# Gate and up in one 512-column product, convolution weights taken one pair at a time, rotary angles started after the convolution

## The chip, the cores and the metric

The kernel runs on one core of a Trainium2 chip. The metric is the device time of one execution in microseconds (us), the median of several runs. TensorE is called PE in the rows, the scalar engine ACT, the vector engine DVE, GpSimd POOL, and SyncE SP; SP issues nearly all loads from DRAM.

## What is computed

A decoder of two layers on 256 tokens of width 1024, all in float32. The parts that the change touches:

```python
def short_conv_mixer(h, w_in, w_conv, w_out):      # layer 0
    b_gate, c_gate, u = jnp.split(h @ w_in, 3, axis=-1)
    z = c_gate * u
    conv = lax.conv_general_dilated(z, w_conv[:, None, :], ...)   # 3 taps, each channel by itself
    return (b_gate * conv) @ w_out

def swiglu(h, w_gu, w_down):                       # both layers, D_FF = 2816
    g, u = jnp.split(h @ w_gu, 2, axis=-1)
    return (jax.nn.silu(g) * u) @ w_down

def rope_cos_sin(positions):                       # used by the attention of layer 1
    ang = positions[..., None] * inv_freq
    return jnp.cos(ang)[:, :, None, :], jnp.sin(ang)[:, :, None, :]
```

Around them stand RMS norms, an attention to a memory of 256 tokens in each layer (keys and values from the memory), and a causal attention in layer 1. Most of the work is the product of 256 tokens with weight matrices: 3 M weights in the convolution's `w_in`, 5.8 M in each layer's `w_gu`.

## The kernel before

**Three products for one.** Every float32 number is split in a part `hi` that TensorE reads exactly and a rest `lo`. A product is then hi by lo, lo by hi and hi by hi, summed in PSUM. Activations are split once. Weights stream: a 512 KB chunk is loaded to one of 5 `raw` buffers, ACT casts it to `hi`, DVE subtracts to get `lo`, and the pair stays in one of 10 buffers until its products are issued. The load of a chunk waits for the `lo` of the chunk five places ahead of it, which frees the raw buffer.

**Two forms.** Where the output has features on the partitions (`mm_cols`: the convolution's `cu` and `pb`, most of the gate and up products `gu`), a weight block is loaded into the array, and one product of 512 columns covers the activations' hi and lo; a second of 256 columns covers the weight's lo. Where the output has tokens on the partitions (`mm_rows`, `gate_up_rows`), 128 tokens are loaded and the weights stream through in three products (`mm3`). The gate and up products of the first two pairs of feature blocks (`ROW_PAIRS` = 2, `jp` 0 and 1) are made in the rows form in each layer, for the tokens of half 0 and then of half 1, so that half 0 can start before half 1 of the FFN's input is normed. There each `mm3` has 256 columns: 8 blocks `k` of the gate, then 8 of the up part, for 2 pairs and 2 halves, which is 2 x 2 x 2 x 8 x 3 = 192 products in a layer. `turn` then makes silu(gate) x up and transposes it back (`pt_g`). The normed input itself is brought to features by transposes (`pt_h`).

**The order of the work** is written by the Python program, instruction by instruction, for engines that each run their queue in order. A `Clock` models when each engine would be done. `side.poll()` after each product lets side jobs (generators that yield the time they want to wait) issue a step, and lets `Feed.pump` issue a cast or a subtraction of the next chunk, if the model has the engine free and its input there. `feed.take(name)` hands out a chunk, and issues at once its cast and subtraction, and those of the chunks ahead of it, where the pump has not done so. `hold` and `grab` wait for one of two PSUM tiles of a kind.

**The convolution** (`short_conv`) has four blocks `jp` of 256 features, in two groups `jj` each. A group is 8 products of 512 columns with `wc` (to one PSUM tile `cu`), 8 with `wu` (to the other), one with `wb` (to `pb`), 24 of 256 columns with the lo of the three, and the last seven with `wb`: 24 of 512 and 24 of 256. ACT and DVE then add the halves of the two `cu` tiles to `conv` tiles in SBUF, and the tiles come free for the next group. All six chunks of a block are taken at its head. The input of the convolution is `mix`: each half of the normed x is transposed (`pt_h`), cast (ACT `mix`) and subtracted (DVE `mix`). Into the first group also falls the job `tables`, which loads gains and the taps of the convolution (`g_rows`, `cw_rows`), transposes them on PE (`pt_c`) and copies them to SBUF.

**The angles** (`angles`) are a side job started ahead of the convolution: a DMA of the positions (`pos_i`), some ten small DVE operations on 32 columns (`ang`, `turns`, `cosang`), and four Sin on ACT (`cs`), ahead of which ACT loads its table for Sin.

Of the kernel before, what the change touches and what calls it, by code (L numbers as in the profile page):

```python
# [19 lines left out]
P = 128  # L20
D = 1024
KD = D // P
T = 256
# [84 lines left out]
class Side:  # L108
# [47 lines left out]
    def hold(self, kind):  # L156

        free = self.free[kind]
        while not free or min(free) > self.clock.now:
            yield 0 if not free else min(free) - self.clock.now  # L160
        free.remove(min(free))
# [11 lines left out]
class Feed:  # L173
# [3 lines left out]
    def __init__(self, clock, items, load, high, low):  # L177
        self.clock, self.items, self.load, self.high, self.low = clock, items, load, high, low
        self.loaded = self.highs = self.lows = self.taken = self.freed = 0
        self.raw, self.ready = {}, {}  # L180
        self.hooks = {}
        self.limit = 5
# [16 lines left out]
    def next_low(self):  # L199
        n = self.lows  # L200
        self.low(self.items[n], self.raw.pop(n), *self.ready[n])
        self.lows += 1
        self.load_to(self.lows + RAWS)
# [51 lines left out]
def yoco_kernel(  # L255
# [51 lines left out]
    def tok(h):  # L307
        return slice(h * P, (h + 1) * P)
# [22 lines left out]
    def load(dst, src, queue=None):  # L331
        (queue or nc.sync).dma_start(dst, src)
        clock.free["dma"] = max(clock.free["dma"], clock.now + 1100)
        clock.note("dma", 1.43 * math.prod(dst.shape[1:]), [dst], [], 900)
# [11 lines left out]

    def load_chunk(it):
        raw = raws.tile([P, it["a"], it["b"]], F32, tag="raw", name=f"raw_{it['name']}")
        src = it["src"].rearrange("(a p) n -> p a n", p=P)
        n = it["b"] // it["pieces"]  # L350
        for i in range(it["pieces"]):
            load(raw[:, :, i * n:(i + 1) * n], src[:, :, i * n:(i + 1) * n])
        return raw
# [36 lines left out]
    def ffn_plan(l):  # L390
        steps, last = ffn_steps()
        plan = []
        for kind, jp in steps + [("down", jp) for jp in last]:
            if kind == "gu":
                plan += col_plan(f"wg{l}_{jp}", ffn_w_gu[l], jp * T)
                plan += col_plan(f"wu{l}_{jp}", ffn_w_gu[l], DFF + jp * T)
            else:
                for k in (2 * jp, 2 * jp + 1):
                    plan.append(dict(name=f"wd{l}_{k}", src=ffn_w_down[l][k * P:(k + 1) * P, :], a=1, b=D,
                                     gain=None, pieces=1, halves=2))  # L400
        return plan
# [206 lines left out]
    def start_rstd():  # L608
        yield 9000
# [194 lines left out]
    def angles():  # L804
# [6 lines left out]
        yield 15000  # L811
# [62 lines left out]
    def short_conv(act, into):  # L874
# [35 lines left out]
        for jp in range(4):  # L910
            wc, wu, wb = ([feed.take(f"{name}_{jp}_{g}") for g in range(2)] for name in ("wc", "wu", "wb"))
            for jj in range(2):
# [3 lines left out]
                for w in (wc, wu):  # L916
                    side.grab("gu")
                    cus.append(gu_tile("cu"))
                    mm_cols(cus[-1], act, w, jj, 0)
                pb = acc_tile("pb").rearrange("p (r t) -> p r t", r=2)  # L920
                mm_cols(pb, act, wb, jj, 0, (0,))
                for i, w in enumerate((wc, wu)):
                    mm_cols(cus[i], act, w, jj, 1)
# [119 lines left out]
    def swiglu(l, src, done, fine_end=False, at_end=None):  # L1043
# [21 lines left out]
        def gate_up_rows(jp, w, h):  # L1065
# [3 lines left out]
            for part in range(2):  # L1069
                for k in range(KD):  # L1070
                    act.need(k, (h,))
                    mm3(gu[:, part, :], act.parts(k, tok(h)), [r[:, k % 4, :] for r in w[part][k // 4]],
                        k == 0, k == KD - 1)
                    side.poll()
# [66 lines left out]
        first = [gu_w(jp) for jp in range(ROW_PAIRS)]  # L1141
# [195 lines left out]
    side.start(angles())  # L1337
    side.finish(x_job[0])
    short_conv(in_mix.act, in_mem0)
    memv0 = mem_values("memv0", mT0)  # L1340
# [28 lines left out]
```

## Time and profile before

| | before |
|---|---|
| median of 3 runs | 802.57 us (801.74 to 802.96) |
| profiled execution, its own time | 804.97 us |
| its span in the trace | 803.2 us |
| PE busy | 789.1 us (98%) |
| DVE, ACT busy | 532.7 us (66%), 436.8 us (54%) |
| mean granted TensorE clock | 0.993 of full speed |
| bytes moved, mean rate | 146.55 MB, 182 GB/s |

"Busy" of PE counts the time from a product's start to its modelled end, and products overlap; the distance of two starts tells more than a duration. A row in brackets `[2.20 <-DVE mix]` says that the engine sat idle for 2.20 us before the instruction, and that DVE's `mix` ended the wait. The granted clock of a stretch is given in parts of full speed.

### The profile page before, as it was taken

To read this page: it belongs to the slowest core of one execution; us is meant where nothing else is said; L and a number is where in the kernel's file an instruction comes from. 1 tells how busy PE (TensorE), PEld (TensorE's weight loads), DVE (VectorE), ACT (ScalarE), POOL (GpSimd) and SP (SyncE) were. 2 spreads that over 40 slices of the span, in tenths; PEclk is the share of its full clock that TensorE was granted. 3 is DMA by queue.
4 is the path that set the end of the run, shared out by engine and by line. 5 is a ranking of instruction groups with operands and counts; after the bars stand their busy time and mean duration, and the time that the engine had idled before them with its cause. 6 is when DMAs were issued, how large, how long until landed. Compare 5 with 4: busy or idle time off the path is not lost.

```text
span 803.2 us, 11672 instructions
## 1 busy us (share of the span) xinstructions
PE 789.1 (98%) x4477; PEld 690.6 (86%) x4477; DVE 532.7 (66%) x830; ACT 436.8 (54%) x727; POOL 17.8 (2%) x44
## 2 busy tenths in 40 slices
PE   8899999999999999999999999999999999999996
PEld 8888788898898888888888889888989988888885
DVE  5888788666756656665765667877757555665553
ACT  6656646565645445554655664556645544554442
POOL 0100001000000000000010000010000000000000
PEclk9999999999999999999999999999999999999999
DMA  9666685833536654666474535667344465466611
GB/s 332 196 191 213 215 269 190 280 136 105 173 97 224 213 185 157 188 212 208 153 236 172 170 106 168 226 206 243 119 121 155 156 212 180 158 203 214 209 55 53
DMA packets 91085, 146.55 MB, mean 182 GB/s; under 512 B 4941, under 2 KB 70549, under 8 KB 90773
## 3 DMA queue, kind: packets, MB, share of 16 engines
q1 hardware_dynamic: 90276, 142.92, 54.8%
q0 software_dynamic: 288, 2.10, 0.7%
q8 instruction: 35, 0.57, 0.3%
q10 hardware_dynamic: 464, 0.79, 0.3%
q14 instruction: 22, 0.17, 0.1%
HBM read 142.64 MB, written 3.15 MB: 182 GB/s over the span
## 4 chain that ended last, share of the span: by engine, by line
PE 88%; DMA 5%; DVE 3%; ACT 2%; issue 1%; SPq 0%; POOLq 0%; ACTq 0%; DVEq 0%
PE gu L315 30%; PE ff L315 14%; PE q_acc L315 6%; PE acc_memv L315 5%; PE acc_mo L315 5%; PE acc_memk L315 3%; PE acc_v L315 3%; PE acc_q L315 3%; PE acc_k L315 3%; PE acc_o L315 3%; PE acc_cout L315 3%; PE cu L315 2%; DMA raw_wu<-in_conv_w_in_dram 2%; PE po L315 2%; PE s L315 2%
## 5 line engine op out<-in xcount | busy, mean ns | idle before, releaser
L315 PE MATMUL ff<-hi_wd,guT 128*128 128x512 f32 (+1 forms) x352 | 107.6, 387 | 0.0
L103 DVE TENSOR_TENSOR gu_sb<-gu_sb,gu 128x256 f32<-128x256 f32 x72 | 30.1, 421 | 97.0 <-ACT gu_sb L103 96.2
L103 ACT COPY gu_sb<-gu 128x256 f32<-128x256 f32 x72 | 26.4, 371 | 101.6 <-PE gu L315 101.5
L315 PEld LDWEIGHTS ff<-hi_wd,guT 128*128 128x128 f32 x352 | 65.9, 188 | 12.2
L103 ACT CAST hi_wu<-raw_wu 128x1024 fp32r<-128x1024 f32 x52 | 54.6, 1050 | 33.5 <-DMA raw_wu<-in_ffn_w_gu_dram 23.0
L315 PE MATMUL gu<-ffn,hi_wg 128*128 128x512 f32 x288 | 71.9, 391 | 0.4 <-DVE gu_sb L103 0.4
L315 PE MATMUL gu<-ffn,hi_wu 128*128 128x512 f32 x288 | 71.2, 389 | 0.0
L315 PE MATMUL ff<-lo_wd,guT 128*128 128x512 f32 (+1 forms) x176 | 68.5, 389 | 0.0
L103 DVE TENSOR_TENSOR lo_wu<-raw_wu,hi_wu 128x1024 fp32r<-128x1024 f32 x52 | 62.8, 1219 | 4.6 <-ACT hi_wu L103 4.5
L315 PEld LDWEIGHTS gu<-ffn,hi_wu 128*128 128x128 f32 x288 | 54.1, 188 | 11.3
L315 PEld LDWEIGHTS gu<-ffn,hi_wg 128*128 128x128 f32 x288 | 53.6, 188 | 11.6 <-DVE gu_sb L103 0.8
L103 DVE TENSOR_TENSOR lo_wd<-raw_wd,hi_wd 128x1024 fp32r<-128x1024 f32 x44 | 53.1, 1219 | 0.0
L103 DVE TENSOR_TENSOR lo_wg<-raw_wg,hi_wg 128x1024 fp32r<-128x1024 f32 x44 | 52.2, 1219 | 0.7 <-ACT hi_wg L103 0.5
L103 ACT CAST hi_wd<-raw_wd 128x1024 fp32r<-128x1024 f32 x44 | 45.6, 1050 | 2.8 <-DMA raw_wd<-in_ffn_w_down_dram 2.8
L315 PE MATMUL acc_memk<-mT,hi_memk 128*128 128x256 f32 x256 | 46.7, 287 | 0.0
L103 ACT CAST hi_wg<-raw_wg 128x1024 fp32r<-128x1024 f32 x44 | 44.6, 1051 | 0.6 <-PE acc_mo L315 0.6
L315 PEld LDWEIGHTS gu<-ffn,lo_wg 128*128 128x128 f32 x288 | 39.3, 190 | 2.8
L315 PE MATMUL acc_mo<-hi_mo,oT_mem 128*128 128x512 f32 x128 | 41.2, 397 | 0.2 <-DVE oT_mem L103 0.2
L315 PE MATMUL gu<-ffn,lo_wu 128*128 128x256 f32 x288 | 40.4, 283 | 0.0
L315 PE MATMUL gu<-ffn,lo_wg 128*128 128x256 f32 x288 | 40.2, 282 | 0.0
L315 PE MATMUL acc_memv<-hi_memv,mT 128*128 128x512 f32 x128 | 39.7, 391 | 0.0
L315 PEld LDWEIGHTS acc_memk<-mT,hi_memk 128*128 128x128 f32 x256 | 39.5, 193 | 0.2
(230 smaller groups left out, 1722.3 us busy)
## 6 DMA issues: line engine op xcount, KB each, us to landing
raw_wg<-in_ffn_w_gu_dram SPq DMA_DIRECT2D x44, 512.0 KB, 5.7
raw_wu<-in_ffn_w_gu_dram SPq DMA_DIRECT2D x44, 512.0 KB, 3.6
raw_wd<-in_ffn_w_down_dram SPq DMA_DIRECT2D x44, 512.0 KB, 4.8
raw_memv<-in_mem_w_kv_dram SPq DMA_DIRECT2D x16, 512.0 KB, 4.9
raw_mq<-in_mem_w_q_dram SPq DMA_DIRECT2D x16, 512.0 KB, 5.3
raw_mo<-in_mem_w_o_dram SPq DMA_DIRECT2D x16, 512.0 KB, 5.4
raw_memk<-in_mem_w_kv_dram SPq DMA_DIRECT2D x14, 512.0 KB, 5.4
raw_wc<-in_conv_w_in_dram SPq DMA_DIRECT2D x8, 512.0 KB, 3.8
```

The lines of the kernel that those rows point to most:

```text
L103: return call(out, *args, **kw)
L315: nc.tensor.matmul(o, l, r, start=start, stop=stop)
```

## The change

It has five parts. (1) In the rows form, the chunks of a pair hold two blocks `k` with 256 gate columns and 256 up columns side by side (`pair_plan`, names `wr`), each loaded by two DMAs of 256 KB. One `mm3` of 512 columns per `k` replaces two of 256, and the chunks are taken as `k` reaches them. (2) `short_conv` takes `wc`, `wu` and `wb` of a block one after the other, each ahead of its first product. (3) The modelled clock lets a load start only when its raw buffer is freed (`emptied`), and has a slower rate for chunks of several blocks; `hold` looks a second time at the clock. (4) The job that norms the memory yields 7000 instead of 9000 ns. (5) `angles` is started behind the convolution and waits 4000 instead of 15000 ns.

```diff
     def hold(self, kind):
         free = self.free[kind]
-        while not free or min(free) > self.clock.now:
+        seen = None
+        while not free or min(free) > self.clock.now != seen:
+            seen = self.clock.now if free else None
             yield 0 if not free else min(free) - self.clock.now
...
         self.lows += 1
+        self.emptied = self.clock.last
         self.load_to(self.lows + RAWS)
...
-    def load(dst, src, queue=None):
+    def load(dst, src, queue=None, rows=True, freed=0.0):
         (queue or nc.sync).dma_start(dst, src)
-        clock.free["dma"] = max(clock.free["dma"], clock.now + 1100)
-        clock.note("dma", 1.43 * math.prod(dst.shape[1:]), [dst], [], 900)
+        clock.free["dma"] = max(clock.free["dma"], clock.now + 1100, freed + 1100)
+        clock.note("dma", (1.43 if rows else 1.9) * math.prod(dst.shape[1:]), [dst], [], 900)
...
+    def pair_plan(name, w, c0):
+        return [dict(name=f"{name}_{g}", a=2, b=2 * T, gain=None, pieces=1, halves=1,
+                     src=[w[g * 256:(g + 1) * 256, c:c + T] for c in (c0, DFF + c0)]) for g in range(4)]
...
-            if kind == "gu":
+            if kind == "gu" and jp < ROW_PAIRS:
+                plan += pair_plan(f"wr{l}_{jp}", ffn_w_gu[l], jp * T)
+            elif kind == "gu":
...
     def start_rstd():
-        yield 9000
+        yield 7000
...
     def angles():
...
-        yield 15000
+        yield 4000
...
         for jp in range(4):
-            wc, wu, wb = ([feed.take(f"{name}_{jp}_{g}") for g in range(2)] for name in ("wc", "wu", "wb"))
+            taken = {}
+            def conv_w(name):
+                if name not in taken:
+                    taken[name] = [feed.take(f"{name}_{jp}_{g}") for g in range(2)]
+                return taken[name]
             for jj in range(2):
...
-                for w in (wc, wu):
+                for name in ("wc", "wu"):
                     side.grab("gu")
                     cus.append(gu_tile("cu"))
-                    mm_cols(cus[-1], act, w, jj, 0)
+                    mm_cols(cus[-1], act, conv_w(name), jj, 0)
                 pb = acc_tile("pb").rearrange("p (r t) -> p r t", r=2)
+                wb = conv_w("wb")
                 mm_cols(pb, act, wb, jj, 0, (0,))
...
             gu = gu_tile("gu")
-            for part in range(2):
-                for k in range(KD):
-                    act.need(k, (h,))
-                    mm3(gu[:, part, :], act.parts(k, tok(h)), [r[:, k % 4, :] for r in w[part][k // 4]],
-                        k == 0, k == KD - 1)
-                    side.poll()
+            both = gu.rearrange("p a t -> p (a t)")
+            for k in range(KD):
+                act.need(k, (h,))
+                if k // 2 == len(w):
+                    w.append(feed.take(f"wr{l}_{jp}_{k // 2}"))
+                mm3(both, act.parts(k, tok(h)), [r[:, k % 2, :] for r in w[k // 2]], k == 0, k == KD - 1)
+                side.poll()
...
-    side.start(angles())
     side.finish(x_job[0])
     short_conv(in_mix.act, in_mem0)
+    side.start(angles())
     memv0 = mem_values("memv0", mT0)
```

How this moves instructions is seen at three places. The first is ACT around the first group of the convolution: `mix_1` is the cast of the second half of the transposed input, `hi_wu` and `hi_wb` are casts of weights, `memk_u` belongs to the memory's keys. Before:

```order
L103 CAST hi_wu_1_486<-raw_wu_1_443 128x1024
L103 CAST mix_0_292<-pt_h 128x4x128
L103 CAST memk_u_482<-k_sb 128x2x256
L103 CAST hi_wb_0_517<-raw_wb_0_462 128x1024
L103 CAST mix_1_293<-pt_h 128x4x128
L103 CAST hi_wb_1_562<-raw_wb_1_501 128x1024
```

The same place of the changed kernel:

```order
L103 CAST hi_wu_0_484<-raw_wu_0_402 128x1024
L103 CAST memk_u_489<-k_sb 128x2x256
L103 CAST mix_1_297<-pt_h 128x4x128
L103 CAST hi_wu_1_523<-raw_wu_1_453 128x1024
L103 CAST hi_wb_0_556<-raw_wb_0_461 128x1024
L103 CAST memk_u_489<-k_sb 128x2x256
L103 CAST hi_wb_1_588<-raw_wb_1_506 128x1024
```

The last `mix_1` stood behind `hi_wb_0`, and stands now two casts of weights earlier, ahead of `hi_wu_1`. On PE the transposes `pt_c` come five products later than before, behind the second product with `hi_wu_1`.

The second place is DVE between the third block of the convolution and the fourth: `conv` adds the halves of the two `cu` tiles of a group, and `lo_wu_0` frees the raw buffer into which `wu_0` of the next block is loaded. Before:

```order
L103 TENSOR_TENSOR lo_wc_1_815<-raw_wc_1_774,hi_wc_1_814 128x1024
L103 TENSOR_TENSOR conv_870<-conv_870,cu 128x256
L103 TENSOR_TENSOR conv_871<-conv_871,cu 128x256
L103 TENSOR_TENSOR conv_870<-conv_870,conv_871 128x256
L103 TENSOR_TENSOR lo_wu_0_833<-raw_wu_0_777,hi_wu_0_832 128x1024
L103 TENSOR_TENSOR lo_wu_1_854<-raw_wu_1_780,hi_wu_1_853 128x1024
```

The same place of the changed kernel:

```order
L103 TENSOR_TENSOR lo_wc_1_805<-raw_wc_1_746,hi_wc_1_804 128x1024
L103 TENSOR_TENSOR yT_562<-conv_752,yT_562 128x256
L103 TENSOR_TENSOR lo_wu_0_831<-raw_wu_0_767,hi_wu_0_830 128x1024
L103 TENSOR_TENSOR conv_838<-conv_838,cu 128x256
L103 TENSOR_TENSOR lo_wu_1_853<-raw_wu_1_782,hi_wu_1_852 128x1024
L103 TENSOR_TENSOR conv_839<-conv_839,cu 128x256
```

`lo_wu_0` stood behind the additions of the group in front of it, and stands now ahead of them. On ACT the load of the Sin table and the four Sin stood ahead of the copies of `conv_870` and `conv_871`, and stand now ahead of the first evacuation of the memory's values. What follows on ACT for the first group of the fourth block, before:

```order
L103 CAST hi_wc_1_993<-raw_wc_1_951 128x1024
L103 CAST hi_wu_0_1007<-raw_wu_0_958 128x1024
L103 COPY conv_969<-cu 128x256
L103 COPY conv_970<-cu 128x256
L103 CAST hi_wu_1_1034<-raw_wu_1_961 128x1024
```

And in the changed kernel:

```order
L103 CAST hi_wc_1_949<-raw_wc_1_879 128x1024
L103 CAST yT_562<-conv_839 128x256
L103 CAST hi_wu_0_969<-raw_wu_0_902 128x1024
L103 COPY conv_927<-cu 128x256
L103 COPY conv_928<-cu 128x256
L103 CAST hi_wu_1_996<-raw_wu_1_923 128x1024
```

The cast `hi_wu_0` still stands ahead of the two copies that bring the `cu` tiles free.

The third place is PE in the rows form of the FFN, layer 0 (`ffn_0` holds the input's blocks 0 to 3, `ffn_1` blocks 4 to 7). Before, from the gate to the up part of the first pair:

```order
L315 MATMUL gu<-lo_wg_0_1_2105,ffn_1_2221 128x256
L315 MATMUL gu<-hi_wg_0_1_2104,ffn_1_2221 128x256 x2
L315 MATMUL gu<-lo_wu_0_0_2176,ffn_0_2220 128x256
L315 MATMUL gu<-hi_wu_0_0_2175,ffn_0_2220 128x256 x2
L315 MATMUL gu<-lo_wu_0_0_2176,ffn_0_2220 128x256
```

In the changed kernel, from the first pair's last block to the second pair:

```order
L319 MATMUL gu<-lo_wr_0_3_2213,ffn_1_2229 128x512
L319 MATMUL gu<-hi_wr_0_3_2212,ffn_1_2229 128x512 x2
L323 MATMUL pt_h<-ident,hn 128x128 x4
L319 MATMUL gu<-lo_wr_1_0_2254,ffn_0_2228 128x512
L319 MATMUL gu<-hi_wr_1_0_2253,ffn_0_2228 128x512 x2
L323 MATMUL pt_g<-ident,gg 128x128 x2
```

A product has 512 columns, and there are half as many; the transposes `pt_h` of the second half's input follow right behind the first pair, and `pt_g` of that pair three products later.

## Rows read from the trace of the kernel before

**Rows 1.** The page, busy time by engine (busy us, share of the span, instructions), and the chain of work that ended last, by engine.

```profile
PE 789.1 (98%) x4477; PEld 690.6 (86%) x4477; DVE 532.7 (66%) x830; ACT 436.8 (54%) x727; POOL 17.8 (2%) x44
...
PE 88%; DMA 5%; DVE 3%; ACT 2%; issue 1%; SPq 0%; POOLq 0%; ACTq 0%; DVEq 0%
```

**Rows 2.** The waits of PE over the whole span: what it waited for, us in total, times, the longest.

```profile
PE cu L315 <- DVE mix L103: 2.2, 1, 2.2
PE cu L315 <- DVE conv L103: 2.1, 1, 2.1
```

**Rows 3.** The timeline of PE in the convolution, the starts of groups and what follows the two waits (start us, us, engine, line, operation, out<-in, shapes, count, idle time before); the last row is the first product behind the convolution.

```profile
33.74 1.09 PE L315 MATMUL cu<-mix,hi_wc 128*128 128x512 f32 x4
37.04 1.21 PE L315 MATMUL cu<-mix,hi_wc 128*128 128x512 f32 x4 [2.20 <-DVE mix L103]
...
38.75 3.28 PE L315 MATMUL cu<-mix,hi_wu 128*128 128x512 f32 x7
...
46.58 1.98 PE L315 MATMUL cu<-mix,hi_wc 128*128 128x512 f32 x8
...
71.60 1.98 PE L315 MATMUL cu<-mix,hi_wc 128*128 128x512 f32 x8
...
82.21 3.33 PE L315 MATMUL cu<-mix,hi_wc 128*128 128x512 f32 x8 [2.11 <-DVE conv L103]
...
92.28 1.98 PE L315 MATMUL cu<-mix,hi_wc 128*128 128x512 f32 x8
...
108.97 0.39 PE L315 MATMUL acc_cout<-lo_cout,yT 128*128 128x512 f32 x1
```

**Rows 4.** Windows of the convolution (stretch, length, then busy us and instructions of PE, weight loads, DVE, ACT, POOL; granted clock, DMA share, GB/s): behind the first wait, an undisturbed stretch, behind the second wait, and the last two groups.

```profile
37.04:42.00 4.96, 4.96 (x15) 3.75 (x16) 4.96 (x5) 1.75 (x3) 0.00 (x0) 0.66 0.43 124
...
50.40:67.10 16.70, 16.70 (x97) 14.77 (x96) 14.56 (x34) 9.46 (x16) 0.00 (x0) 1.00 0.53 162
...
82.00:88.00 6.00, 5.79 (x19) 4.67 (x20) 5.58 (x11) 2.31 (x5) 0.00 (x0) 0.72 0.19 57
...
92.30:109.00 16.70, 16.70 (x98) 14.78 (x97) 13.38 (x23) 9.45 (x17) 0.00 (x0) 1.00 0.92 293
```

**Rows 5.** Timelines of ACT and of DVE ahead of the first wait.

```profile
34.73 1.04 ACT L103 CAST hi_wb<-raw_wb 128x1024 fp32r<-128x1024 f32 x1 [2.50 <-DMA raw_wb<-in_conv_w_in_dram]
35.68 0.58 ACT L103 CAST mix<-pt_h 128x512 fp32r<-128x512 f32 x1
...
36.29 0.69 DVE L103 TENSOR_TENSOR mix<-pt_h,mix 128x512 fp32r<-128x512 f32 x1 [2.13 <-ACT mix L103]
...
39.77 2.35 DVE L103 TENSOR_TENSOR lo_wb<-raw_wb,hi_wb 128x1024 fp32r<-128x1024 f32 x2
```

**Rows 6.** The chain of work through the second wait, in order of time (start us, us, what).

```profile
68.50 1.28 ACT L103
...
70.67 0.76 DVE conv L103 x2
...
72.94 1.23 DVE lo_wu L103
74.22 6.14 DMA raw_wu<-in_conv_w_in_dram
...
81.33 0.38 ACT conv L103
81.73 0.43 DVE conv L103
```

**Rows 7.** Timeline of SP: the issues of the small loads around the start of the convolution, and the page's row on the load of the positions (KB, us from issue to landing). Then PE's transpose of the taps.

```profile
33.60 0.30 SPq L332 DMA_DIRECT2D cw_rows<-in_conv_w_dram  x1
...
pos_i<-in_positions_dram SPq DMA_DIRECT2D x1, 1.0 KB, 3.5
...
38.54 0.28 PE L319 MATMUL pt_c<-ident,cw_rows 24*128 24x24 f32 x1
```

**Rows 8.** Windows of the rows form of the FFN in layer 0 and layer 1 (columns as in rows 4).

```profile
213.25:237.76 24.51, 24.51 (x207) 24.51 (x206) 14.27 (x21) 11.51 (x18) 0.55 (x1) 1.00 0.38 119
610.15:634.67 24.52, 24.52 (x207) 24.51 (x206) 14.18 (x21) 11.51 (x18) 1.40 (x1) 1.00 0.37 118
```

**Rows 9.** Pieces of the chain: 48 products of 256 columns in the rows form of the FFN, 50 of 512 columns in the rows form of the convolution's output product, and a run of 16 of 512 and of 16 of 256 columns in the convolution.

```profile
227.53 5.75 PE gu L315 x48
...
109.13 11.34 PE acc_cout L315 x50
...
92.45 3.63 PE cu L315 x16
96.30 1.91 PE cu L315 x16
```

**Rows 10.** Timelines ahead of the memory's values: DVE's last subtraction of their weights, and ACT's first evacuation of them; then DVE in the rows form of the FFN, its norm of the second half and the gate of the first pair.

```profile
137.39 1.28 DVE L103 SCALAR_TENSOR_TENSOR lo_memv<-raw_memv,g_cols,hi_memv 128x1024 fp32r<-128x1024 f32 x1
...
143.06 1.31 ACT L103 ACTIVATE memv<-acc_memv,m_rs 128x512 fp32r<-128x512 f32 x2 [5.99 <-PE acc_memv L315]
...
218.11 1.41 DVE L103 SCALAR_TENSOR_TENSOR hn<-x_sb,rs,g_ffn 128x512 f32<-128x512 f32 x2
...
219.61 0.43 DVE L103 TENSOR_TENSOR gg<-gu,sg 128x256 f32<-128x256 f32 x1
```

More of the change, by code (lines that the diff above doesn't have):

```diff
@@ L180, in __init__ @@
         self.raw, self.ready = {}, {}
+        self.emptied = 0.0
         self.hooks = {}
@@ L345, in col_plan @@
                      halves=2) for g in range(2)]
+    def pair_plan(name, w, c0):
+        return [dict(name=f"{name}_{g}", a=2, b=2 * T, gain=None, pieces=1, halves=1,
+                     src=[w[g * 256:(g + 1) * 256, c:c + T] for c in (c0, DFF + c0)]) for g in range(4)]
     def load_chunk(it):
         raw = raws.tile([P, it["a"], it["b"]], F32, tag="raw", name=f"raw_{it['name']}")
[L349 to L352, printed above, removed]
+        if isinstance(it["src"], list):
+            parts = it["src"]
+        else:
+            n = it["b"] // it["pieces"]
+            parts = [it["src"][:, i * n:(i + 1) * n] for i in range(it["pieces"])]
+        n = it["b"] // len(parts)
+        for i, src in enumerate(parts):
+            load(raw[:, :, i * n:(i + 1) * n], src.rearrange("(a p) n -> p a n", p=P), rows=it["a"] == 1,
+                 freed=feed.emptied)
         return raw
@@ L915, in short_conv @@
                 jobs, cus = [], []
-                for w in (wc, wu):
+                for name in ("wc", "wu"):
                     side.grab("gu")
                     cus.append(gu_tile("cu"))
-                    mm_cols(cus[-1], act, w, jj, 0)
+                    mm_cols(cus[-1], act, conv_w(name), jj, 0)
                 pb = acc_tile("pb").rearrange("p (r t) -> p r t", r=2)
+                wb = conv_w("wb")
                 mm_cols(pb, act, wb, jj, 0, (0,))
-                for i, w in enumerate((wc, wu)):
-                    mm_cols(cus[i], act, w, jj, 1)
+                for i, name in enumerate(("wc", "wu")):
+                    mm_cols(cus[i], act, conv_w(name), jj, 1)
                     if jj:
@@ L1139, in down @@
                 side.poll()
-        first = [gu_w(jp) for jp in range(ROW_PAIRS)]
+        first = [[] for _ in range(ROW_PAIRS)]
         for h in range(2):
```

## The prediction, made before the changed kernel had run

> **What bounds the kernel now.** The page comes first: PE is busy for 98% of the span, and the chain that ended last is PE for 88% [rows 1]. So there are two ways to gain: fewer or shorter products, or the removal of PE's waits. The list of PE's waits says where these are: two of 2.2 and 2.1 us, both ahead of a product for `cu`, so both in the convolution [rows 2].
>
> The timeline of PE in the convolution shows what they cost in all [rows 3]. Its eight groups are equal work. From 46.58 to 71.60 there are three, at 8.34 us each, and the last two take from 92.28 to 108.97, 8.345 each. The first takes 46.58 − 33.74 = 12.84, so 4.50 more. The two groups from 71.60 to 92.28 take 20.68, so 4.00 more. That is 8.5 us, twice the idle time of 4.3. The windows show the rest: right behind the waits the granted clock is 0.66 and 0.72, and 1.00 in an undisturbed stretch [rows 4]; a part of each stretch runs at the lower level, 1.2 GHz, and seven products take 3.28 us [rows 3] where 16 take 3.63 [rows 9].
>
> What each wait hangs on is read from ACT, DVE and the chain. The first: DVE's `mix` at 36.29 waits for ACT's `mix` at 35.68, which needs only transposes, but stands in ACT's queue behind `hi_wb`, and that had waited 2.50 us for its load until 34.73 [rows 5]. The second goes through a load: the Sin table (68.50, 1.28 us) delays the copies that DVE adds (70.67), `lo_wu` stands behind these additions and ends at 74.2, and only then is the raw buffer free for `raw_wu` of the next block, which takes 6.14 us; ACT casts it and makes its copies at 81.33, DVE adds at 81.73, and a `cu` tile is free for PE at 82.21 [rows 6].
>
> **The change part by part.**
>
> *First wait.* The order of ACT puts the last `mix_1` ahead of `hi_wu_1` and `hi_wb_0`, so it no longer waits for `raw_wb`. The wait goes, and with it the slow stretch: −4.50. What is late next? The transposes `pt_c` need `cw_rows`, which is issued at 33.60. Before, PE came to them at 38.54, 4.9 us later, and no wait is shown [rows 7], so the load takes at most 4.9; the positions, as small, took 3.5 [rows 7]. In the changed order 14 products stand ahead of `pt_c`; at 3.63/16 = 0.227 us [rows 9] PE is there at 33.74 + 3.2 = 36.9. The taps land between 37.1 and 38.5, some 0.5 later if SP's issues slip: a wait of 0.2 to 2.1 us. I take 0.7, nearer the lower end, since the positions' load is the like of it. The other subtractions of this stretch come close to their use: `lo_wb` ended at 39.77 + 2.35 = 42.1 before [rows 5], and PE, no longer late, needs its second half near 40. DVE's chain moves ahead by the wait that it lost (2.13 [rows 5]), so about as much as PE asks. I take 0.5, between 0 and 1.5. Net −3.3.
>
> *Second wait.* The table load and the Sin leave this place, and `lo_wu_0` stands ahead of the additions on DVE. These additions belong to a group that starts at 63.26 (46.58 + 2 x 8.34) less the 3.3 gained, and its first `cu` is complete after 16 products of 512 columns, one for `pb` and 8 of 256: 16 x 0.227 + 0.227 + 8 x 0.119 = 4.8 us [rows 9], at 64.8. So `lo_wu_0` ends by about 66, the load starts there and not at 74.2, and lands at 66 + 6.1 = 72.1; its cast ends at 73.2. The copies behind it need the first `cu` of the next group, which is complete at 71.60 − 3.3 + 4.8 = 73.1. So nothing is left of the wait, if the load takes no longer than it did. So −4.00; a load that lands one microsecond later delays the copies and PE by about as much. In all the convolution gains 8.5 − 1.2 = 7.3.
>
> *Rows form.* 192 products of 256 columns become 96 of 512 in a layer. 48 of 256 take 5.75 us, 119.8 ns each; 50 of 512 with weights streaming in the same form take 11.34, 226.8 each [rows 9]. A pair becomes cheaper by 2 x 119.8 − 226.8 = 12.8 ns, 96 of them by 1.23 us; the stage of 24.51 us [rows 8] should take 23.3, and both layers together gain 2.5. Against it, `pt_g` now comes earlier: in layer 0 at 213.25 + 24 x 0.227 = 218.69, and the `pt_h` and three products behind, at about 219.8. Its input `gg` stands on DVE behind the norm `hn` and a subtraction. `hn` ended at 219.5 [rows 10]; in the changed order one subtraction fewer (1.2 us) is ahead of it, so 218.3; with the subtraction 219.5, with `gg` 219.9. I price this edge at 0.1 in all; if `hn` gained nothing, it would be 1.3 a layer. Net −2.4.
>
> How much of a pair is saved is the fixed share of a product, and these rows put it at 12.8 ns: 119.8 for 256 columns and 226.8 for 512 leave 107.0 for 256 more columns [rows 9]. The Trainium skill (TensorE: Matmul & The Clock Gate, section Back-to-back issue gap) gives N/2.4 + 2.5 ns for a single warm product of N columns. By that rule a pair would gain 2.5 ns, 0.5 us in all and not 2.5; the rows agree with its slope of 106.7 ns for 256 columns and not with its fixed share, and the sum goes by the rows.
>
> *Loads of the pairs.* Each chunk has two DMAs in place of one, 16 more issues for the two layers. SP's issue took 0.30 us [rows 7]; DMA is at a share of 0.38 in these stages and DVE is busy for 14.3 of 24.5 us [rows 8], which hides it. Without that cover it is 16 x 0.3 = 4.8 us. Nothing is taken.
>
> *Angles.* The table (1.28 us [rows 6]) and four Sin now stand where ACT idles 5.99 us ahead of the first evacuation of the memory's values [rows 10]. On DVE eight small operations of about 0.2 us come ahead of the last `lo_memv`, which ended at 138.7 [rows 10]; PE needs it for the last six products ahead of that evacuation, at 143.06 − 6 x 0.227 = 141.7, so 3.0 us less 1.6 remain. Nothing is taken; up to 0.5.
>
> *Clock model, `hold`, the norm's earlier start* only move instructions, which the order above has in it.
>
> The sum is −7.3 − 2.4 = −9.7 against the profiled execution's 804.97: 795.3. That execution is 2.4 above the median of the runs, so the median goes from 802.57 to **792.9**.
>
> **The rivals.**
>
> *One wait stays or moves* (0.20): the load of the taps comes late, or the fourth block's `hi_wu_0`, which still stands ahead of the copies on ACT, waits for its load. For it: the casts of weights are in one queue with the evacuations, and a load took 6.1 to 6.7 us. A wait of 2.1 with its slow stretch costs 4.0 to 4.5 [rows 3], so 792.9 + 4 = 797.
>
> *The supply is the limit, and the waits only move* (0.07): loads follow raw buffers, and the last two groups draw 293 GB/s at a DMA share of 0.92 [rows 4]. But from 50.40 to 67.10 PE works without a gap at 0.53 [rows 4]. Then only the rows form gains: 800.1.
>
> *The 512-column product saves nothing* (0.06): only columns count, and the transposes and hand-overs that come with a pair take back the fixed share. For it: the edge at `pt_g` can cost 1.3 us a layer, as much as the products gain. Against it: 226.8 ns of `acc_cout`, under twice 119.8 [rows 9]. This gives 792.9 + 2.4 = 795.3. The rule of the Trainium skill's page on TensorE named above would put it 0.5 lower.
>
> *Slower* (0.04): `take` issues a cast and a subtraction at the point of use if the pump has not. Taking `wu` and `wb` late then exposes two casts and a subtraction, 2 x 1.04 + 1.2 = 3.3 us, less what PE has queued (8 products, 1.8): 1.5 us at each of 8 takes, 12 us, so about 805. It decides from 9.7/8 = 1.2 us a take on. Against it: in the changed order the casts of `wu` stand ahead of the products by several others.
>
> **How the numbers follow.** The main case has 0.63, and a range of its own from 791 to 794.5: taps and `lo_wb` give −1.0 at their lower ends, and one of them or the angles gives +1.5 at the upper. Range 790.5 to 797.5: it takes in the one wait that stays, the edge at `pt_g` with 2.6, and the short gain, and leaves out the supply limit, the slower case and the upper tail of a stay (0.07 + 0.04 + 0.06). A difference under 0.2% (1.6 us) can hardly be told from none. Faster 0.92, same 0.04, slower 0.04.
>
> **What would show it.** In the changed profile the eight groups should stand 8.34 us apart but for the first, which has 1 to 2 more; no wait for `mix` and none for `conv`; a granted clock of 0.9 or above in the first windows; a wait of `pt_c` on its loads of under a microsecond. The rows stages should take 23.3 us, their products 227 ns apart. The Sin should run ahead of the evacuation of the memory's values, and PE should not wait there. Any stretch with a granted clock near 0.7 in the convolution would say that a wait stayed, and a stage of 24.2 us that the product was mis-sized.

## The result, and the profile after

The changed kernel takes 795.78 us (median of 4 runs, 795.54 to 796.09), the kernel before 802.15 (4 runs, 800.34 to 802.96): a ratio of 0.9924, with an interval from 0.9906 to 0.9942. That is 6.1 us faster by the ratio, where 9.7 were forecast; the forecast of 792.9 lies 2.9 us below the result. The profiled execution of the changed kernel took 796.02 us, though, with a span of 794.2, and against the profiled execution of before (804.97, span 803.2) the sum had said 795.3. So the two profiles differ by 9.0 us and the medians by 6.4, and this is the main thing to explain.

The waits of PE after. Neither wait of [rows 2] is left; what is new is one for DVE's `gg` in the rows form, once in each layer. A third wait of before, behind the rows form of layer 1, is gone too; its row comes first, then the rows of after.

```profile
PE gu L315 <- DVE gu_sb L103: 0.4, 1, 0.4
...
PE pt_g L323 <- DVE gg L103: 0.4, 2, 0.2
PE pt_m L323 <- DMA m<-in_mem_dram: 0.2, 1, 0.2
PE acc_mo L319 <- DVE oT_mem L103: 0.2, 1, 0.2
```

PE's timeline in the convolution, the answer to [rows 3], and the window of its first group (columns as in [rows 4]):

```profile
34.21 2.00 PE L319 MATMUL cu<-mix,hi_wc 128*128 128x512 f32 x8
36.05 1.52 PE L319 MATMUL cu<-mix,hi_wu 128*128 128x512 f32 x6
...
37.59 0.21 PE L323 MATMUL pt_c<-ident,cw_rows 24*128 24x24 f32 x1
37.73 0.73 PE L319 MATMUL cu<-mix,hi_wu 128*128 128x512 f32 x2
...
43.02 1.98 PE L319 MATMUL cu<-mix,hi_wc 128*128 128x512 f32 x8
...
68.04 1.98 PE L319 MATMUL cu<-mix,hi_wc 128*128 128x512 f32 x8
...
93.06 1.98 PE L319 MATMUL cu<-mix,hi_wc 128*128 128x512 f32 x8
...
101.40 0.39 PE L319 MATMUL acc_cout<-lo_cout,yT 128*128 128x512 f32 x1
```

```profile
34.21:43.02 8.81, 8.81 (x53) 7.51 (x51) 8.54 (x13) 4.94 (x7) 0.00 (x0) 1.00 0.84 264
```

The first group takes 8.81 us, and from 43.02 to 101.40 seven groups take 8.34 each. The convolution takes 67.19 us; it took 75.23 in [rows 3]. The granted clock of the first group is 1.00. What the first group has above 8.34 lies at the two transposes `pt_c`: six products from 36.05 end at 37.41, the next one starts at 37.73, 0.32 later, and the rest of the 0.47 comes right behind. No wait is shown there.

The place of the second wait, on DVE, SP and ACT, the answer to [rows 6]:

```profile
63.58 1.22 DVE L103 TENSOR_TENSOR lo_wu<-raw_wu,hi_wu 128x1024 fp32r<-128x1024 f32 x1
...
65.50 1.22 DVE L103 TENSOR_TENSOR lo_wu<-raw_wu,hi_wu 128x1024 fp32r<-128x1024 f32 x1
...
66.78 2.29 SPq L336 DMA_DIRECT2D raw_wu<-in_conv_w_in_dram  x2
...
71.65 1.05 ACT L103 CAST hi_wu<-raw_wu 128x1024 fp32r<-128x1024 f32 x1 [0.84 <-DMA raw_wu<-in_conv_w_in_dram]
73.10 0.37 ACT L103 COPY conv<-cu 128x256 f32<-128x256 f32 x1 [0.40 <-PE cu L319]
```

The load is issued 7.4 us earlier than before, its cast ends at 72.7, and the copy behind the cast waits for PE, not for the cast. Two names ahead of the prediction have to be set right here. The load is issued behind the second of the two subtractions, `lo_wu_1`: it ended at 66.72, and before at 74.17 [rows 6]. So `lo_wu_1`, and not `lo_wu_0`, frees the buffer into which `wu_0` of the next block is loaded. And only these loaded weights are the fourth block's: the additions that delayed `lo_wu` are those of the second block's last group, and the copies behind the cast are those of the third block's first group, which starts at 71.60 before and at 68.04 after.

The windows of the rows form in both layers, the answer to [rows 8]:

```profile
205.69:229.69 24.00, 23.82 (x111) 19.25 (x110) 14.36 (x22) 11.51 (x18) 1.46 (x1) 1.00 0.44 131
601.95:625.97 24.02, 23.84 (x111) 19.24 (x110) 14.38 (x22) 11.51 (x18) 1.40 (x1) 1.00 0.43 131
```

They take 0.5 us less each, and 1.2 were forecast. PE's timeline behind the first pair, and DVE's at the same time, show where the rest stays:

```profile
211.13 0.60 PE L323 MATMUL pt_h<-ident,hn 128*128 128x128 f32 x4
...
211.80 0.63 PE L319 MATMUL gu<-hi_wr,ffn 128*128 128x512 f32 x2
212.61 0.44 PE L323 MATMUL pt_g<-ident,gg 128*128 128x128 f32 x2 [0.18 <-DVE gg L103]
212.80 0.48 PE L319 MATMUL gu<-lo_wr,ffn 128*128 128x512 f32 x1
213.21 0.65 PE L323 MATMUL pt_h<-ident,hn 128*128 128x128 f32 x4
...
211.00 1.22 DVE L103 TENSOR_TENSOR lo_wg<-raw_wg,hi_wg 128x1024 fp32r<-128x1024 f32 x1
212.13 0.42 DVE L103 TENSOR_TENSOR gg<-gu,sg 128x256 f32<-128x256 f32 x1
212.47 0.68 DVE L103 TENSOR_TENSOR ffn<-pt_h,ffn 128x512 fp32r<-128x512 f32 x1
```

The 24 products ahead, from 205.69 to 211.13, take 5.44 us, 226.7 ns each, as priced. Two products behind 211.80 leave PE free at 212.25, and `pt_g` starts at 212.61, since `gg` stands behind `lo_wg` on DVE. Then one product takes from 212.80 to 213.21, 0.18 more than its 0.23: the second `pt_h` needs the PSUM tile that `ffn` gives back at 213.15. The bracket of 0.18 shows only a part of the first wait, and none of the second: it counts from a product's modelled end.

By stage the two profiles differ so (us, from the first product of each stage to the next):

| stage | before | before, profiled again | after |
|---|---|---|---|
| start, to the first product of the memory's keys | 6.90 | 6.75 | 6.54 |
| memory's keys | 26.84 | 27.46 | 27.67 |
| convolution | 75.23 | 71.14 | 67.19 |
| output product to memory's output | 104.28 | 104.30 | 104.29 |
| rows form, layer 0 | 24.51 | 24.51 | 24.00 |
| column form of layer 0 to layer 1's attention | 372.39 | 372.49 | 372.26 |
| rows form, layer 1 | 24.52 | 24.52 | 24.02 |
| rest | 168.53 | 168.53 | 168.23 |
| span | 803.2 | 799.7 | 794.2 |

The middle column is the first experiment.

### The profile page after: what moved, and what is told of

It is laid out like the page before. It is cut to its first block, busy times and chain, and to the rows that moved or that the text cites. A ratio compares the mean times of both kernels' runs of the same rounds, so it can differ in the third digit from the quotient of the medians.

```text
span 794.2 us, 11303 instructions
## 1 busy us (share of the span) xinstructions
PE 784.7 (99%) x4285; PEld 678.8 (85%) x4285; DVE 531.7 (67%) x830; ACT 435.7 (55%) x727; POOL 18.0 (2%) x44
## 3 DMA queue, kind: packets, MB, share of 16 engines
HBM read 142.64 MB, written 3.15 MB: 184 GB/s over the span
## 4 chain that ended last, share of the span: by engine, by line
PE 97%; DVE 1%; DMA 0%; POOL 0%; issue 0%; ACT 0%; POOLq 0%; DVEq 0%; ACTq 0%
PE gu L319 29%; PE ff L319 15%; PE acc_memk L319 6%; PE q_acc L319 6%; PE cu L319 6%; PE acc_memv L319 5%; PE acc_mo L319 5%; PE pb L319 3%; PE acc_v L319 3%; PE acc_q L319 3%; PE acc_k L319 3%; PE acc_o L319 3%; PE acc_cout L319 3%; PE po L319 2%; PE s L319 2%; PE pt_h L323 1%
## 5 line engine op out<-in xcount | busy, mean ns | idle before, releaser
L103 DVE TENSOR_TENSOR lo_wu<-raw_wu,hi_wu 128x1024 fp32r<-128x1024 f32 x44 | 53.5, 1219 | 1.1 <-ACT hi_wu L103 1.0
L103 ACT CAST hi_wu<-raw_wu 128x1024 fp32r<-128x1024 f32 x44 | 46.2, 1051 | 2.3 <-DMA raw_wu<-in_conv_w_in_dram 2.3
L103 DVE TENSOR_TENSOR lo_wg<-raw_wg,hi_wg 128x1024 fp32r<-128x1024 f32 x36 | 42.7, 1219 | 1.6 <-ACT hi_wg L103 1.6
L319 PE MATMUL gu<-hi_wr,ffn 128*128 128x512 f32 x128 | 39.8, 392 | 0.0
```

The source lines that it names most:

```text
L103: return call(out, *args, **kw)
L319: nc.tensor.matmul(o, l, r, start=start, stop=stop)
```

## The experiments

**The kernel before, once more.** No edit.

> The kernel before, unchanged, profiled a second time. Theory A: what the two waits of the convolution cost differs from execution to execution, because each hangs on a load; the profiled execution of 804.97 us had more of it than the median run. Then this profile has its excess over 8 undisturbed groups (66.7 us) at another value than the 8.5 us of the first, and its total differs from 804.97 by about as much. Theory B: the two waits are fixed by the order of the instructions, and the 2.4 us between the profiled execution and the median lie elsewhere (start, end, recording). Then the convolution takes 75.2 us again, whatever the total is.

Median 801.78 of 10 runs (800.20 to 804.49), ratio to the kernel before 0.9999 (0.9983 to 1.0014). The profiled execution took 801.52. PE's timeline, then the window behind the first wait, then ACT's timeline ahead of the second, of the first profile and of this one:

```profile
37.47 1.19 PE L315 MATMUL cu<-mix,hi_wc 128*128 128x512 f32 x4 [2.17 <-DVE mix L103]
38.51 0.40 PE L315 MATMUL cu<-mix,hi_wu 128*128 128x512 f32 x1
...
39.06 1.90 PE L315 MATMUL cu<-mix,hi_wu 128*128 128x512 f32 x7
...
79.94 2.11 PE L315 MATMUL cu<-mix,hi_wc 128*128 128x512 f32 x8 [0.89 <-DVE conv L103]
```

```profile
37.47:42.00 4.53, 4.53 (x24) 3.63 (x25) 4.53 (x5) 1.78 (x3) 0.00 (x0) 1.00 0.46 126
```

```profile
80.38 1.04 ACT L103 CAST hi_wu<-raw_wu 128x1024 fp32r<-128x1024 f32 x1 [2.82 <-DMA raw_wu<-in_conv_w_in_dram]
...
78.11 1.05 ACT L103 CAST hi_wu<-raw_wu 128x1024 fp32r<-128x1024 f32 x1 [1.15 <-DMA raw_wu<-in_conv_w_in_dram]
```

The convolution takes 71.14 us: its excess over eight groups of 8.34 (66.72) is 4.4 us, where it was 8.5. The first wait is as long as before (2.17 for 2.20), but the clock stays at 1.00 behind it, and the seven `hi_wu` products take 1.90 us in place of 3.28 [rows 3]. The second is 0.89 in place of 2.11. The cast of `hi_wu` waits for its load in both profiles, and that load, issued at 73.44 and at 74.22, was ready after 4.67 us here and after 6.16 in the first profile. Theory A holds: the spans differ by 3.5 us, with 4.1 less in the convolution and 0.5 more at the start and in the keys. The 0.32 us at `pt_c` are here too: the product at 38.51 ends its 0.23 at 38.74, and the next starts at 39.06. Over all executions measured beside the experiments, before took 798.9 to 806.2 us; the changed kernel, without such waits, took 795.2 to 796.2.

**The changed kernel, once more**, beside the next two on one chip. No edit.

> The changed kernel, unchanged, beside the others on one chip. Both theories: about 795.8 us, convolution 67.2 us, rows stages 24.0 us each. It is the measure for the two runs that follow.

Median 795.50 of 6 runs (795.21 to 796.21); convolution 67.19, rows forms 23.99 and 24.00 us.

**Without the 512-column products.** `pair_plan` and the loop of `gate_up_rows` as before, the rest changed:

```diff
-                mm3(both, act.parts(k, tok(h)), [r[:, k % 2, :] for r in w[k // 2]], k == 0, k == KD - 1)
...
+            for part in range(2):
+                for k in range(KD):
+                    act.need(k, (h,))
+                    mm3(gu[:, part, :], act.parts(k, tok(h)), [r[:, k % 4, :] for r in w[part][k // 4]],
+                        k == 0, k == KD - 1)
```

> The changed kernel with the gate and up products of the first pairs made as before (256 columns, separate chunks); all else changed. The order in the convolution is then that of the changed kernel. Theory of the edge: the 512-column products save 1.2 us a layer, and 0.6 to 0.7 of it is lost again at the transposes, so this run is 1.0 us slower than the changed kernel (796.8), with rows stages of 24.5 us. Rival, the columns alone count: the same stages and times as the changed kernel within 0.3 us.

Median 797.30 (797.09 to 798.00), 1.8 us above the changed kernel on the same chip. The windows of the rows form:

```profile
205.96:230.48 24.52, 24.52 (x207) 24.51 (x206) 14.18 (x21) 11.50 (x18) 1.46 (x1) 1.00 0.39 119
603.17:627.69 24.52, 24.52 (x208) 24.52 (x207) 14.18 (x21) 11.50 (x18) 1.39 (x1) 1.00 0.36 118
```

1.0 of the 1.8 us are these two stages, as the theory of the edge had it. The spans of the two profiles differ by 2.0 us: besides these 1.0, 0.4 lies between the two stages (372.69 against 372.26), 0.8 in the start and the keys, which differ from execution to execution, and −0.2 at the end. The rival falls. As this kernel has all the edits of the convolution, its distance to the kernel before on the same chip (802.43 us) is what they bring at the median: 5.1 us.

**Further chunks held back from DVE.** `Feed.pump` issues nothing from the sixth `k` of the first pair until `gg` is written:

```diff
     def pump(self, soon):
+        if self.quiet:
+            return
...
+                if (h, jp, k) == (0, 0, 5):
+                    feed.quiet = True
...
                 gg = times(sg, gu[:, 1, :])
+                feed.quiet = False
```

> The changed kernel with the casts and subtractions of further chunks held back from the sixth block k of the first pair until DVE has made its gg. DVE then makes gg right behind the norm, and the subtraction lo_wg comes behind it. Theory of the edge: the wait of the transposes pt_g (0.36 us from the end of the products ahead of them to their start) goes, and the second pt_h, which waits for DVE's ffn, comes up to 0.2 earlier or stays; the rows stages take 23.4 to 23.7 us, and the total falls by 0.6 to 1.2 us against the changed kernel. Rival: the loss at the transposes is a cost of the transposes among 512-column products; the stages stay at 24.0.

Median 795.80 (795.02 to 796.28) beside the changed kernel's 795.50: no gain. The rows forms take 23.92 and 23.95 us, more than the 23.4 to 23.7 that were expected. The list of waits has another one in place of that for `gg`:

```profile
PE pt_h L326 <- DVE ffn L103: 0.5, 2, 0.2
```

The stages stay near the rival's 24.0, but not by its cause: the wait for `gg` went, and came back as one for the PSUM tile of the first `pt_h`.

**The second `pt_h` later as well.** The same, and one line in `Normed.run`:

```diff
                 yield from turn_parts(hns[g], self.act, h, g)
                 side.give("half")
+                if (h, g) == (1, 0) and self.name.startswith("ffn"):
+                    yield 900
```

> The changed kernel with the further chunks held back as in the run before it, and the second pt_h of the second half written 900 ns later, eight products behind the first pt_h and not four. It waited for the PSUM tile that the first pt_h gives back (DVE's ffn). Theory, two waits at this place, for gg and for the tile: both go, the rows stages take 23.4 us, 0.6 us a layer less than in the changed kernel; the median falls to 794.3. Rival, the transposes among products of 512 columns cost it without a wait: the stages stay at 23.9.

Median 794.66 (793.78 to 795.45), the lowest of all kernels here. It was timed on another chip than the changed kernel, and against the kernel before on the same chip the ratio is 0.9912, where the changed kernel has 0.9914; so a gain at the median is not shown, but the stages are clear. The windows of the rows form:

```profile
206.66:230.17 23.51, 23.51 (x111) 19.24 (x110) 14.47 (x22) 11.52 (x18) 1.46 (x1) 1.00 0.43 134
602.38:625.87 23.49, 23.49 (x111) 19.25 (x110) 14.47 (x22) 11.50 (x18) 1.40 (x1) 1.00 0.42 135
```

PE is busy for the whole stage, and each takes 0.5 us less than in the changed kernel. Both waits are shown: for `gg`, and for the tile behind it. (The later `pt_h` alone, without holding back the chunks, was not run.) What is left to 24.52 − 1.23 = 23.29 is 0.2 us a layer.

**One edit alone, and one edit undone.** Four edits move the instructions of the convolution, and these runs take them one by one. First the norm's earlier start alone (`yield 9000` to `yield 7000`):

> The kernel before with one edit: the memory's norm yields 7000 and not 9000 ns. The written order of ACT then has the last mix ahead of hi_wb_0; the Sin table stays in the convolution. Theory, one wait for each place: the wait for mix goes with its slow stretch, 3.0 to 4.5 us, and the wait for conv stays at what it takes in an execution, 1 to 4 us; the first group takes 8.3 to 9.5 us, the median falls by 3 to 4 us. Rival, the supply is the limit: the wait only moves to a later group, and the median stays within 1 us of before.

Median 800.50, ratio 0.9983 (0.9970 to 0.9995). The profiled execution took 798.52, the lowest of ten, and its convolution 69.72 us. The first group took 8.80 us: the wait for `mix` went. The one for `conv` is there, split in two, at the same group and two groups later:

```profile
78.41 2.11 PE L315 MATMUL cu<-mix,hi_wu 128*128 128x512 f32 x8 [0.85 <-DVE conv L103]
...
94.37 2.11 PE L315 MATMUL cu<-mix,hi_wc 128*128 128x512 f32 x8 [0.79 <-DVE conv L103]
```

The median fell by 1.6 us, where the theory had 3 to 4 and the rival at most 1: the first wait goes, as the theory had it, and a part of the gain is lost again at a wait that came later, as the rival had it. Then the angles alone (started behind the convolution, `yield 4000`):

> The kernel before with one edit: the angles started behind the convolution. ACT's order around the first group is that of before, so the wait for mix stays (2.2 us, the group 11.3 to 12.8). No Sin table in the convolution, and lo_wu of the third block now stands ahead of the additions on DVE. Theory: the wait for conv goes, the groups behind the first are 8.34 us apart, the median falls by 1.5 to 4 us. Rival, the supply: a wait of 1 us or more at another group.

Median 799.26, ratio 0.9971 (0.9953 to 0.9990); convolution 69.76 us. The wait for `mix` stays and the one for `conv` is gone, so the theory holds (the groups behind the first stand 8.34 to 8.48 apart). The edit takes the table, the four Sin and the small DVE operations out of the stage together; which of them counts, no run tells.

```profile
36.94 1.20 PE L315 MATMUL cu<-mix,hi_wc 128*128 128x512 f32 x4 [1.92 <-DVE mix L103]
```

The changed kernel with the angles back ahead of the convolution:

> The changed kernel with the angles started ahead of the convolution as before; all else changed. The Sin table stands then in the convolution's third block, while the chunks are taken one after the other. Theory, the table delays the load of the next block's wu through the additions and subtractions: a wait for conv of 1 to 2 us comes back, 1.5 to 4 us slower than the changed kernel. Rival, the late taking of the chunks alone removes that wait, since lo_wu stands ahead of the additions in this order too: as fast as the changed kernel within 0.5 us.

Median 796.93, ratio to before 0.9944 (0.9922 to 0.9965), 1.2 us above the changed kernel, on another chip; convolution 68.69. Neither theory nor rival: a wait came back, but for `lo_wb`, one block earlier. The table is not its cause, since its load starts only at 59.78, behind the wait. On DVE nine small operations of the angles, 1.7 us in all, now stand ahead of `lo_wb` in this block; it starts at 56.39, and in the changed kernel at 54.54 (last row). That they make the wait is read from the order, and not shown by a run.

```profile
57.67 0.73 PE L319 MATMUL pb<-mix,lo_wb 128*128 128x256 f32 x4 [0.58 <-DVE lo_wb L103]
58.80 0.74 PE L319 MATMUL pb<-mix,lo_wb 128*128 128x256 f32 x4 [0.40 <-DVE lo_wb L103]
...
56.39 2.35 DVE L103 TENSOR_TENSOR lo_wb<-raw_wb,hi_wb 128x1024 fp32r<-128x1024 f32 x2
...
59.78 1.28 ACT L103 ACT_TABLE_LOAD   x1
...
54.54 2.35 DVE L103 TENSOR_TENSOR lo_wb<-raw_wb,hi_wb 128x1024 fp32r<-128x1024 f32 x2
```

The chunks taken all at a block's head again, the rest changed (`wc, wu, wb` from one line ahead of the loop over `jj`):

> The changed kernel with all six chunks of a block of the convolution taken at its head, as before. In the written order mix stands ahead of hi_wb as in the changed kernel, and there is no Sin table in the stage. Theory, the two waits were removed by the order around mix and by the table's absence, and taking the chunks late adds nothing of its own: convolution 67.2 to 67.6 us, total as the changed kernel within 0.5 us (795.0 to 796.0). Rival, taking the chunks one after the other is what removes the second wait: a wait of 1 us or more for conv or lo_wb, 797 or more.

Median 795.78 (795.29 to 796.11), convolution 67.19: the same as the changed kernel. Taking the chunks one after the other brings nothing here of its own. Alone, on the kernel before, it was this:

> The kernel before with one edit: the chunks of the convolution taken one after the other. ACT's order around the first group is that of before, so the wait for mix stays (1.9 to 2.2 us, 2.7 to 4.5 with what follows). The Sin table stays in the stage, but lo_wu of the third block stands between the additions on DVE and no longer behind both. Theory, the table and that order make the second wait together: it shrinks to 0 to 1 us, the median is 0 to 2 us below before. Rival, late taking exposes casts: waits for lo_wu or lo_wb, the median is above before.

Median 805.56 (803.02 to 807.11), ratio 1.0033 (1.0012 to 1.0054): slower, as the rival had it. The timelines of ACT, DVE and PE in the second block, then the window behind the wait:

```profile
57.85 1.05 ACT L103 CAST hi_wc<-raw_wc 128x1024 fp32r<-128x1024 f32 x1 [3.80 <-DMA raw_wc<-in_conv_w_in_dram]
58.81 0.50 ACT L103 ACTIVATE conv<-conv,cw 128x256 f32<-128x256 f32 x1
...
59.34 1.00 DVE L103 SCALAR_TENSOR_TENSOR conv<-conv,cw,conv 128x255 f32<-128x255 f32 x2 [2.87 <-ACT conv L103]
...
60.83 1.22 DVE L103 TENSOR_TENSOR lo_wu<-raw_wu,hi_wu 128x1024 fp32r<-128x1024 f32 x1
...
62.10 1.22 PE L315 MATMUL cu<-mix,lo_wu 128*128 128x256 f32 x4 [3.15 <-DVE lo_wu L103]
```

```profile
62.00:68.10 6.10, 6.00 (x19) 5.05 (x20) 4.08 (x9) 1.60 (x3) 0.00 (x0) 0.52 0.76 233
```

A cast in ACT's queue waits 3.80 us for its load; the convolution's `conv` stands behind it, DVE's `conv` behind that, `lo_wu` behind that, and PE waits. It isn't a cast at the point of use, as the prediction's slower rival had it, but a cast written too early. Now the modelled clock undone, the rest changed:

> The changed kernel with the modelled clock of before (the slower rate of loads, the time at which a raw buffer is freed and the second look of hold undone). In the written order mix stands ahead of hi_wb by the norm's earlier start alone. Theory: the two waits stay away, convolution 67.2 to 68 us, 795 to 797 us. Rival, the clock's model of loads is what keeps casts from standing ahead of loads that have not landed: a wait of 1 us or more in the convolution or in a later stage, 797 or more.

Median 796.95, ratio 0.9926 (0.9907 to 0.9946), 1.2 us above the changed kernel and, on the same chip, above the run before this one; convolution 68.61, with a wait of 0.54 for `conv` and one of 0.20 for `g_rows` at `pt_c`. Neither holds: the median is in the theory's range, the convolution above it, and the waits are under the 1 us of the rival. And the modelled clock alone on the kernel before (with the second look of `hold`, left out here):

```diff
+        self.emptied = self.clock.last
...
-        clock.free["dma"] = max(clock.free["dma"], clock.now + 1100)
-        clock.note("dma", 1.43 * math.prod(dst.shape[1:]), [dst], [], 900)
+        clock.free["dma"] = max(clock.free["dma"], clock.now + 1100, freed + 1100)
+        clock.note("dma", (1.43 if rows else 1.9) * math.prod(dst.shape[1:]), [dst], [], 900)
```

> The kernel before with one edit: the modelled clock of the changed kernel (loads of several blocks slower, a load not ahead of its raw buffer, the second look of hold). In the written order mix stands ahead of hi_wb, behind hi_wu_1; the Sin table stays, with lo_wu of the third block behind the additions. Theory, one wait for each place: the wait for mix goes (3 to 4.5 us with what follows), the one for conv stays (1 to 4 us), the median falls by 2 to 4 us. Rival, the edits of the order do not act one by one, since each shifts all casts that follow: a wait at another place, as taking the chunks late alone has shown; the median is within 1 us of before or above.

Median 797.28 (796.55 to 797.94), ratio 0.9937 (0.9920 to 0.9953), convolution 67.39 us: both waits are gone with this edit alone, though the Sin table is still in the stage and `lo_wu` still behind the additions. ACT at the place of the second wait:

```profile
74.12 0.37 ACT L103 COPY conv<-cu 128x256 f32<-128x256 f32 x1 [2.59 <-PE cu L319]
74.39 1.05 ACT L103 CAST hi_wc<-raw_wc 128x1024 fp32r<-128x1024 f32 x1
75.34 0.38 ACT L103 COPY conv<-cu 128x256 f32<-128x256 f32 x1
...
75.91 1.06 ACT L103 CAST hi_wu<-raw_wu 128x1024 fp32r<-128x1024 f32 x1
```

Neither theory nor rival: both waits went, and the median fell by 5.1 us. The copies now stand ahead of `hi_wu`, so the load's delay by the table meets nothing. This part alone brings the convolution to 67.39 us, near the 67.19 of all four, and the other three without it bring it to 68.61. Which of the clock's own three edits does it was not run. The edits don't add: −5.1 (clock), −1.6 (norm), −2.9 (angles) and +3.2 (chunks), by medians, against about −5 for all four of them (the changed kernel without the 512-column products).

## Why the prediction was right, and where it was off

**The two waits.** Right. PE waited neither for `mix` nor for `conv`. The first group took 8.81 us, 0.47 above 8.34 where 1.2 were forecast, but not for the reason given: neither `pt_c` (0.7) nor `lo_wb` (0.5) waited. The 0.47 is time at the transposes `pt_c` that the group had before as well, so of the 4.50 only 4.0 could go. The numbers of the second place came out nearly as walked: load 66.78 (forecast 66), cast 71.65 to 72.7 (72.1 to 73.2), copies 73.10 (73.1). A part of that is luck: `lo_wu_0`, from which the load was counted, ended at 64.80, and the load waited for `lo_wu_1`, which the walk left out. Against the profiled execution the convolution gained 8.04, forecast 7.3.

**The step that failed: from the profile to the median.** The prediction added the 2.4 us by which the profiled execution lay above the median as if they were an offset that any kernel would have. They were part of the waits that the change removes: the same kernel profiled again lost 4.4 us and not 8.5 in the convolution. So the gain of 8.0 in the convolution counts only about 5 at the median, as the run without the 512-column products shows (5.1). The changed kernel, which has no such waits, lay 0.24 us above its median when it was profiled. This is 2.2 of the 2.9 us by which the forecast missed; the other 0.7 is the sum against the profile (796.02 for 795.3). That this is so small is luck: the convolution gained 0.7 more than forecast, and the rows form 1.4 less. The range held the result only by the room that it left for the edge at `pt_g`, a wait that stays and a short gain; the main case's own range ended at 794.5.

**The rows form.** The mechanism was right and the term mis-sized: 2.4 us forecast, 1.0 measured. The products cost 226.7 ns, as priced. By the Trainium skill (TensorE: Matmul & The Clock Gate, section Back-to-back issue gap) a single warm product of 512 columns would cost N/2.4 + 2.5 ns, an estimate of 215.8 ns. This trace doesn't agree: it has 226.7 at a granted clock of 1.00. The bound of 1.3 us a layer for the edge at `pt_g` held, but the value taken (0.1 in both layers) was wrong. `gg` was ready 6.86 us behind the start of the stage and not 6.65, and missed PE by 0.36 us a layer, and behind it a second wait, for the tile that `ffn` gives back, was not in the sum. The runs with the held-back chunks and the later `pt_h` show both.

**Nothing for the angles and the loads of pairs.** Right: the stretch from the output product to the memory's output took 104.28 before and 104.29 after.

**Start and keys.** They took 0.5 us more in the profile of after (34.21 for 33.74). In the other profiles of kernels with all or most of the edits this was 33.7 to 35.2, and part of it is PE's wait for the memory's load at `pt_m` (0.2 to 1.2 us), so it is not settled whether the change costs something here. Over all profiles the convolution starts at 34.5 us on average with the clock's edit (eight profiles) and at 33.9 without it (six), so a cost of half a microsecond is possible, but not shown. 0.4 us that were gained in the column forms and the end were not forecast; most of it lies where before had the wait for `gu_sb`.

**The cause given for the second wait** was incomplete. The load was late behind the table and the additions, and with the angles moved away the wait went; but the delay reached PE only because a cast stood ahead of the copies on ACT. The clock model, which the prediction passed over as an edit that "only moves instructions", puts that cast behind the copies when it is the only edit, and that is enough. In the changed kernel `hi_wu_0` still stands ahead of them, and no wait came because its load landed in time.

**The rivals.** The slower one did not come in the whole change, but the edit that it named, alone, was slower by 0.33%, by another mechanism. The one that a wait stays came only where single edits were made or undone. The one that the 512-column product saves nothing was worth 795.3, close to the result, but did not come: the product saved 1.0 us. The supply is no limit: after, the convolution runs without a gap.

## What to carry to other kernels

Where a wait hangs on a load, one profile shows one draw of it: take a second profile before a gain is added up, and forecast against the median's share of the wait, not the profile's. On engines that run in order, ask of each instruction that waits for a load what stands behind it; a planner that thinks a load early writes the cast too soon, and mending its model of the load may do the work of several edits. When a product gets shorter or denser, what was hidden between products comes due earlier: price the next two waits behind it, not the first alone.

## What the runs showed of the hardware

A wait of the same length had different consequences in two executions of one program. Behind 2.20 us of idle time the granted clock was 0.66 over the next 5 us [rows 4], so partly at the lower of the two levels, and behind 2.17 us it was 1.00. The first group took 4.50 us more than 8.34 in the one and 2.96 in the other, a difference of 1.5 us. Behind 3.15 us, with the chunks taken late, the clock was 0.52, and the group took 6.30 more. Without the 0.47 us of the first group that no wait made, these waits on TensorE cost between 1.1 and 2.0 times the idle time that their rows show, and the program did not fix how much.
